# Every third half chunk's low part on GpSimd instead of VectorE, in a two-layer decoder trunk that streams all its weights

## The chip, the cores and the metric

One core of a Trainium2 chip. The metric is the device time of one execution in microseconds (us): the median of several runs, and beside it one profiled execution with its trace.

## The reference, cut to what matters

The program computes two layers on 256 tokens of width 1024, in float32. Layer 0 mixes with an RG-LRU group and an HGRN2 group, layer 1 with a Mamba-2 scan; each layer then has cross-attention into 256 memory tokens and a squared-ReLU MLP. Nearly all of the arithmetic is products with weights:

```
h = rmsnorm(x, norm_mix_g[l])
proj = h @ e_w_in[e]            (layer 0, 1024 x 6144; layer 1: o_w_in, 1024 x 6176)
x = x + mix                     (mix = ... @ e_w_out[e], 2048 x 1024)
x = x + mem_cross_attn(...)     (four 1024 x 1024 weights)
hf = rmsnorm(x, norm_ffn_g[l])
x = x + jnp.square(jax.nn.relu(hf @ ffn_w1[l])) @ ffn_w2[l]
```

Each weight is used once, against all 256 tokens.

## The kernel before, in words

**Three products for one.** A float32 operand is split into two parts that TensorE takes in a shorter format: the high part is the operand rounded, the low part is what the rounding left. Activations have parts H and L, weights `wh` and `wl`. A product is three matmuls: `wh`x`H`, `wh`x`L`, `wl`x`H` (lines 465, 467, 468 where the weights are the stationary operand, 484 to 486 where the activations are; 1202 to 1204 for the last four halves).

**The weight stream.** The host lays all weights out as 161 chunks of 2048 columns by 128 partitions, in the order in which they are used. Each is loaded and split as two halves of 1024 columns, so there are 322 halves, numbered h = 0 to 321 (the two of chunk `dt` have 512 columns). Class `Stream` takes each half through three steps:

- `loading` (line 155): SyncE's queue issues the DMA of 512 KB into `raw`, of which there are 4 buffers.
- `splitting`, line 169: ScalarE copies `raw` with rounding into `wh`, of which there are 5 buffers.
- `splitting`, line 170: VectorE subtracts `wh` from `raw` into `wl`, of which there are 5 buffers. Both operands lie in SBUF. When this is done the `raw` buffer is free. Halves 0 to 2 are split in two pieces each, so line 170 issues 325 instructions.

When TensorE's products of half h have been written, `ahead` (lines 183 to 188) writes the splits up to half h + 3 and the loads up to h + 7; the buffers allow one more split, since a half can be copied as soon as the half five before it is used up.

**What else VectorE does.** Line 629 is a causal convolution (its input is in PSUM), 1057, 1090, 1088, 1093, 1111, 1112 and 1126 belong to the Mamba-2 scan of one of eight groups, 359 and 388 make low parts of activations, 730 and 731 belong to HGRN2. Lines 303 to 308 are a chain of small instructions for an inverse square root; 316 and 318 turn its result into two diagonal matrices `dgh` and `dgl`, which TensorE multiplies with ones (line 326) to spread the scale over the partitions. The chain of lines 1015 to 1024 (a softplus and a cumulative sum) makes `acT` for the scan, which TensorE transposes at line 1033.

**What sets the order.** The program text gives an order and priorities (the chains above run under `high_priority`); a scheduler writes one fixed list of instructions per engine from it. Each engine works through its own list in order and waits at semaphores. An instruction that stands early in TensorE's list and whose operand is late stops everything behind it.

GpSimd does little: four constants and two memsets (line 673) at the start.

Of the kernel before, what the change touches and what calls it, by code (L numbers as in the profile page):

```python
# [7 lines left out]
F32 = mybir.dt.float32  # L8
# [4 lines left out]
ALU = mybir.AluOpType  # L13
# [117 lines left out]
class Stream:  # L131
# [26 lines left out]
    def splitting(self):  # L158
        h = self.cut
        self.cut += 1  # L160
        nc = self.nc
        hk, n = self._shape(h)
        w = hk * n
        raw = self.raw.pop(h)
        hi = self.pool.tile([P, 1024], F32R, tag="wh", bufs=PART_BUFS, name=f"wh{h // 2}_{h % 2}")
        lo = self.pool.tile([P, 1024], F32R, tag="wl", bufs=PART_BUFS, name=f"wl{h // 2}_{h % 2}")
        self.parts[h] = tuple(t[:, :w].rearrange("p (k c) -> p k c", k=hk) for t in (hi, lo))
        for a, b in self._pieces(h, w):
            self.last = nc.scalar.copy(hi[:, a:b], raw[:, a:b])  # L169
            nc.vector.tensor_tensor(lo[:, a:b], raw[:, a:b], hi[:, a:b].bitcast(F32), ALU.subtract)  # L170
            yield

    def load(self, upto):
# [1128 lines left out]
```

## Time and profile before

| | us |
|---|---|
| median of 3 runs (lowest, highest) | 1012.09 (1011.84, 1013.56) |
| the profiled execution's own time | 1005.65 |
| its span, first to last instruction | 1003.8 |
| TensorE busy | 990.7 |
| VectorE busy | 773.6 |
| ScalarE busy | 615.0 |
| GpSimd busy | 1.2 |

The profiled execution lies 6.4 us under the median; 1.85 us of it lie outside its span. TensorE's busy time is a union of overlapping matmuls, so what it lost inside small waits does not all show as idle. Its granted clock is 0.996 over the span.

### The profile page before, as it was taken

The page shows a single profiled execution, that of the slowest core. Times are in us where ns is not written, and L with a number is a line of the kernel's source. Part 1 is how long each engine was busy: PE and PEld are TensorE (multiplying, and loading weights), DVE is VectorE, ACT ScalarE, POOL GpSimd, SP SyncE. Part 2 cuts the span into 40 slices and gives each one's busy share as a digit, 9 for nine tenths or more (in the row PEclk, how much of TensorE's full clock was granted, in tenths as well). Part 3 has the DMA queues.
Part 4 walks back from the last instruction along what each step waited for, and adds up shares of the span by engine and source line. Part 5 has one row for each costly group of instructions (what it writes and reads, how often), then busy time and mean ns, then how long its engine had stood idle before and what let it go on. Part 6 is the DMA issues. An engine that isn't in the chain of part 4 may idle for free.

```text
span 1003.8 us, 20814 instructions
## 1 busy us (share of the span) xinstructions
PE 990.7 (99%) x8453; PEld 942.1 (94%) x8453; DVE 773.6 (77%) x1459; ACT 615.0 (61%) x907; POOL 1.2 (0%) x6
## 2 busy tenths in 40 slices
PE   9999999999999999999999999999999999999997
PEld 8898998989999999999998999999999999989985
DVE  7968888796887864675798888999989777656653
ACT  6667868775566554455445867778456657535542
POOL 0000000000000000000000000000000000000000
PEclk9999999999999999999999999999999999999999
DMA  8765453545544655555555655554646345666551
GB/s 294 274 218 164 127 188 123 176 148 183 187 147 159 197 190 191 196 198 194 168 172 194 217 196 189 188 156 141 211 137 200 127 159 184 198 192 191 192 188 42
DMA packets 52703, 180.54 MB, mean 180 GB/s; under 512 B 5984, under 2 KB 6144, under 8 KB 52480
## 3 DMA queue, kind: packets, MB, share of 16 engines
q1 hardware_dynamic: 52176, 178.41, 53.9%
q8 instruction: 66, 1.08, 0.4%
q10 hardware_dynamic: 432, 0.80, 0.2%
q14 instruction: 29, 0.24, 0.1%
HBM read 178.11 MB, written 1.08 MB: 179 GB/s over the span
## 4 chain that ended last, share of the span: by engine, by line
PE 84%; DVE 10%; ACT 3%; DMA 2%; issue 1%; SPq 0%; ACTq 0%; DVEq 0%
PE pg L465 20%; PE pg L467 19%; PE pg L468 19%; PE pg L484 6%; PE pg L486 6%; PE pg L485 5%; DVE wl L170 3%; DMA raw<-in_wst_dram 1%; ACT wh L169 1%; DVE cv L629 1%; PE pm L689 1%; PE pm L851 1%; PE pm L852 1%; PE pm L853 1%; DMA mem<-in_memT_dram 1%
## 5 line engine op out<-in xcount | busy, mean ns | idle before, releaser
L169 ACT CAST wh<-raw 128x1024 fp32r<-128x1024 f32 (+1 forms) x325 | 337.0, 1041 | 301.3 <-PE pg L467 205.3
L170 DVE TENSOR_TENSOR wl<-raw,wh 128x1024 fp32r<-128x1024 f32 (+1 forms) x325 | 391.5, 1211 | 164.1 <-ACT wh L169 163.3
L465 PE MATMUL pg<-nh,wh 128*128 128x256 f32 x1280 | 359.6, 281 | 0.0
L467 PE MATMUL pg<-nl,wh 128*128 128x256 f32 x1280 | 355.9, 278 | 0.0
L468 PE MATMUL pg<-nh,wl 128*128 128x256 f32 x1280 | 355.8, 278 | 0.0
L465 PEld LDWEIGHTS pg<-nh,wh 128*128 128x128 f32 x1280 | 241.1, 188 | 1.5 <-issue 0.7
L468 PEld LDWEIGHTS pg<-nh,wl 128*128 128x128 f32 x1280 | 241.3, 189 | 0.0
L467 PEld LDWEIGHTS pg<-nl,wh 128*128 128x128 f32 x1280 | 240.9, 188 | 0.4
L465 PE MATMUL pg<-yh,wh 128*128 128x256 f32 x768 | 215.6, 281 | 0.6 <-ACT wh L169 0.6
L467 PE MATMUL pg<-yl,wh 128*128 128x256 f32 x768 | 214.7, 280 | 0.1
L468 PE MATMUL pg<-yh,wl 128*128 128x256 f32 x768 | 214.3, 280 | 0.0
L465 PEld LDWEIGHTS pg<-yh,wh 128*128 128x128 f32 x768 | 146.1, 190 | 1.8 <-ACT wh L169 1.5
L467 PEld LDWEIGHTS pg<-yl,wh 128*128 128x128 f32 x768 | 145.7, 190 | 0.4 <-DVE yl L388 0.3
L468 PEld LDWEIGHTS pg<-yh,wl 128*128 128x128 f32 x768 | 145.4, 189 | 0.6 <-DVE wl L170 0.5
L486 PE MATMUL pg<-wl,yh 128*128 128x512 f32 x176 | 69.3, 394 | 0.0
L485 PE MATMUL pg<-wh,yl 128*128 128x512 f32 x176 | 69.0, 392 | 0.0
L484 PE MATMUL pg<-wh,yh 128*128 128x512 f32 x176 | 68.7, 391 | 0.0
L629 DVE SCALAR_TENSOR_TENSOR cv<-pg,smC,cv 128x255 f32<-128x255 f32 (+2 forms) x96 | 39.9, 478 | 0.7 <-ACT cv L626 0.7
L484 PEld LDWEIGHTS pg<-wh,yh 128*128 128x128 f32 x176 | 33.0, 188 | 7.4 <-issue 0.3
L485 PEld LDWEIGHTS pg<-wh,yl 128*128 128x128 f32 x176 | 33.1, 188 | 7.2
L486 PEld LDWEIGHTS pg<-wl,yh 128*128 128x128 f32 x176 | 33.1, 188 | 6.7
L943 DVE SCALAR_TENSOR_TENSOR t<-pg,rb 128x512 f32<-128x512 f32 x32 | 21.9, 690 | 13.2 <-PE pg L468 13.0
(266 smaller groups left out, 1105.7 us busy)
## 6 DMA issues: line engine op xcount, KB each, us to landing
raw<-in_wst_dram SPq DMA_DIRECT2D x317, 512.0 KB, 3.7
ac<-acd SPq DMA_DIRECT2D x16, 256.0 KB, 4.5
mem<-in_memT_dram SPq DMA_DIRECT2D x8, 256.0 KB, 4.2
raw<-in_wst_dram SPq DMA_DIRECT2D x8, 256.0 KB, 4.9
xres<-in_xT_dram SPq DMA_DIRECT2D x4, 256.0 KB, 5.8
gw<-in_gatew_dram SPq DMA_DIRECT2D x1, 1024.0 KB, 5.5
gn<-in_fing_dram SPq DMA_DIRECT2D x2, 256.0 KB, 3.7
out_dram<-o SPq DMA_DIRECT2D x2, 256.0 KB, 2.1
```

What stands on the lines that cost most here:

```text
L169: self.last = nc.scalar.copy(hi[:, a:b], raw[:, a:b])
L170: nc.vector.tensor_tensor(lo[:, a:b], raw[:, a:b], hi[:, a:b].bitcast(F32), ALU.subtract)
L465: PE.matmul(o[:, j, :], wh[:, cs], xh, start=(first and k == 0 and j == 0), stop=False, skip_group_check=True)
L467: PE.matmul(o[:, j, :], wh[:, cs], xl, start=False, stop=False, skip_group_check=True)
L468: PE.matmul(o[:, j, :], wl[:, cs], xh, start=False, stop=(last and k == kt - 1), skip_group_check=True)
L484: PE.matmul(os[j], h, wh, start=(first and k == 0), stop=False)
L485: PE.matmul(os[j], lo, wh, start=False, stop=False)
L486: PE.matmul(os[j], h, wl, start=False, stop=(last and k == kt - 1))
L629: V.scalar_tensor_tensor(r[:, j, i:], o[:, j, :256 - i], col(wn, (3 - i) * stride + c), r[:, j, i:], ALU.mult, ALU.add)
L689: PE.matmul(tgt[32 * j:32 * j + 32, b // 4, :], Kf[:, 32 * b:32 * b + 32], qq[:, 32 * b:32 * b + 32], start=True, stop=True, tile_position ...
L851: PE.matmul(o, ah, bh, start=(i == 0), stop=False)
L943: V.scalar_tensor_tensor(t, o, 0.0, b2(n.rb), ALU.max, ALU.mult)
```

## The change

Of every half with h > 8 and h divisible by 3, the subtraction that makes the low part is issued on GpSimd instead of VectorE. These are h = 9, 12, ..., 321, that is 105 of the 322 halves, all of them 1024 columns wide. Nothing else is written differently; the scheduler makes new lists from it. One line is added, so all later lines have numbers one higher.

```diff
         for a, b in self._pieces(h, w):
             self.last = nc.scalar.copy(hi[:, a:b], raw[:, a:b])
-            nc.vector.tensor_tensor(lo[:, a:b], raw[:, a:b], hi[:, a:b].bitcast(F32), ALU.subtract)
+            e = nc.gpsimd if h > 8 and h % 3 == 0 else nc.vector
+            e.tensor_tensor(lo[:, a:b], raw[:, a:b], hi[:, a:b].bitcast(F32), ALU.subtract)
             yield
```

The lists move at other places too. Two of them follow, each for VectorE and TensorE. In the names, the number behind `wl_`, `wh_` or `pm_` is the buffer's number in the program and is the same before and after; `wl_0` and `wl_1` are the first and second half of a chunk.

**Place 1, the transposition of `acT` at the start of layer 1.** VectorE before, the end of the chain (lines 352 to 355) that leads to `acT`:

```order
L352 SCALAR_TENSOR_TENSOR sp_7671<-sp_7671,sp_7668 128x256 x2
L170 TENSOR_TENSOR wl_1_7853<-raw_1_7664,wh_1_7852 128x1024
L352 SCALAR_TENSOR_TENSOR sp_7671<-sp_7671,sp_7668 128x256 x4
L170 TENSOR_TENSOR wl_0_7886<-raw_0_7729,wh_0_7885 128x1024
L353 SCALAR_TENSOR_TENSOR sp_7671<-sp_7671,sp_7670 128x256
L629 SCALAR_TENSOR_TENSOR cv_7815<-pg_7740,smC,cv_7815 128x255
L355 SCALAR_TENSOR_TENSOR sp_7669<-sp_7671,sp_7669 128x256
```

VectorE now, the same chain (its lines are now 353 to 356, and `acT` is made at 1025):

```order
L351 TENSOR_SCALAR sp_7671<-sp_7668 128x256
L353 SCALAR_TENSOR_TENSOR sp_7671<-sp_7671,sp_7668 128x256 x6
L354 SCALAR_TENSOR_TENSOR sp_7671<-sp_7671,sp_7670 128x256
L356 SCALAR_TENSOR_TENSOR sp_7669<-sp_7671,sp_7669 128x256
L171 TENSOR_TENSOR wl_1_7853<-raw_1_7664,wh_1_7852 128x1024
L1022 TENSOR_SCALAR sp_7691<-sp_7669,na 128x256
L1025 SCALAR_TENSOR_TENSOR acT<-smB,sp_7691 128x128 x2
```

`wl_0_7886` and the convolution now stand behind the chain.

TensorE before, where the transposition (line 1033) stands in the products of chunk `z_0`, whose `wh_1_7768` is its second half:

```order
L468 MATMUL pg_7824<-nh_7461,wl_1_7769 128x256
L465 MATMUL pg_7824<-nh_7461,wh_1_7768 128x256
L467 MATMUL pg_7824<-nl_7462,wh_1_7768 128x256
L1033 MATMUL pm_7807<-smB,acT 128x32
L468 MATMUL pg_7824<-nh_7461,wl_1_7769 128x256
```

TensorE now, the same transposition (line 1034), with `wh_0_7725`, the first half of that chunk:

```order
L469 MATMUL pg_7740<-nh_7461,wl_1_7661 128x256
L466 MATMUL pg_7824<-nh_7359,wh_0_7725 128x256
L468 MATMUL pg_7824<-nl_7360,wh_0_7725 128x256
L1034 MATMUL pm_7807<-smB,acT 128x32
L469 MATMUL pg_7824<-nh_7359,wl_0_7726 128x256
```

It stands 40 rows earlier in TensorE's list (4012 instead of 4052).

**Place 2, the scale of group 5 of the scan (`dgh_10248`, `pm_10346`).** VectorE before, ahead of `dgh`:

```order
L170 TENSOR_TENSOR wl_1_10486<-raw_1_10225,wh_1_10485 128x1024
L306 SCALAR_TENSOR_TENSOR nt_10236<-nt_10235 128x2
L170 TENSOR_TENSOR wl_0_10524<-raw_0_10285,wh_0_10523 128x1024
L307 TENSOR_TENSOR nt_10236<-nt_10236,nt_10234 128x2
L170 TENSOR_TENSOR wl_1_10600<-raw_1_10344,wh_1_10599 128x1024
L308 SCALAR_TENSOR_TENSOR nt_10235<-nt_10236,nt_10235 128x2
L359 TENSOR_TENSOR kv_11139<-vN_8340,kv_11138 128x512
L316 TENSOR_SCALAR dgh_10248<-smB,nt_10235 128x128 x2
```

VectorE now (303 to 308 are 304 to 309, 316 is 317):

```order
L308 TENSOR_TENSOR nt_10236<-nt_10236,nt_10234 128x2
L1112 SCALAR_TENSOR_TENSOR y_10321<-cv_9773,smB,pm_10309 128x256
L309 SCALAR_TENSOR_TENSOR nt_10235<-nt_10236,nt_10235 128x2
L1113 TENSOR_TENSOR y_10321<-y_10321,z_9974 128x512
L317 TENSOR_SCALAR dgh_10248<-smB,nt_10235 128x128 x2
L319 SCALAR_TENSOR_TENSOR dgl_10249<-smB,nt_10235,dgh_10248 128x128 x2
L336 TENSOR_TENSOR ysq_10354<-ysq_10354 128x256
L360 TENSOR_TENSOR kv_11139<-vN_8340,kv_11138 128x512
```

`wl_1_10486` (h = 231) is on GpSimd now; `wl_0_10524`, `wl_1_10600`, `kv_11139` and one `ysq` stand behind `dgh`. TensorE before, where the products with ones (line 326) stand in chunk `oo_02`:

```order
L468 MATMUL pg_10292<-yh_9096,wl_0_10406 128x256
L465 MATMUL pg_10292<-yh_9096,wh_0_10405 128x256
L326 MATMUL pm_10346<-dgh_10248,onesr 128x256
L1081 MATMUL pm_10376<-cv_10184 128x256
L326 MATMUL pm_10346<-dgl_10249,onesr 128x256
```

TensorE now, in chunk `oo_00`:

```order
L468 MATMUL pg_10290<-yl_9819,wh_1_10221 128x256
L469 MATMUL pg_10290<-yh_9818,wl_1_10222 128x256
L327 MATMUL pm_10346<-dgh_10248,onesr 128x256
L1082 MATMUL pm_10376<-cv_10184 128x256
L327 MATMUL pm_10346<-dgl_10249,onesr 128x256
```

They stand 77 rows earlier (5318 instead of 5395). The same products of groups 6 and 7 stand 71 and 86 rows earlier.

## Rows read from the trace of the kernel before

**Rows 1.** The page's head and its busy times of the engines.

```profile
span 1003.8 us, 20814 instructions
...
PE 990.7 (99%) x8453; PEld 942.1 (94%) x8453; DVE 773.6 (77%) x1459; ACT 615.0 (61%) x907; POOL 1.2 (0%) x6
```

**Rows 2.** Busy time by stretch; columns are named in the first row.

```profile
core 0: us, PE busy (x) PEld busy (x) DVE busy (x) ACT busy (x) POOL busy (x), PEclk, DMA share, GB/s
300.00:500.00 200.00, 200.00 (x1756) 200.00 (x1755) 133.99 (x167) 107.91 (x139) 0.00 (x0) 1.00 0.57 189
500.00:525.00 25.00, 24.61 (x212) 24.21 (x212) 23.70 (x59) 12.12 (x17) 0.00 (x0) 1.00 0.46 151
525.00:550.00 25.00, 23.68 (x173) 22.44 (x172) 22.61 (x51) 13.51 (x19) 0.00 (x0) 0.93 0.60 199
625.00:775.00 150.00, 148.50 (x1277) 143.53 (x1276) 142.03 (x327) 98.78 (x143) 0.00 (x0) 1.00 0.53 169
```

**Rows 3.** Waits of the whole span: total us, times, longest us.

```profile
ACT wh L169 <- PE pg L467: 205.3, 157, 3.4
DVE wl L170 <- ACT wh L169: 163.3, 175, 3.3
...
PE pm L326 <- DVE dgh L316: 1.6, 6, 0.4
PE pm L1033 <- DVE acT L1024: 1.3, 1, 1.3
```

**Rows 4.** Timeline 400 to 412: start us, duration us, instruction, [idle before, releaser].

```profile
400.74 1.05 ACT L169 CAST wh<-raw 128x1024 fp32r<-128x1024 f32 x1 [1.67 <-PE pg L467]
...
401.83 1.23 DVE L170 TENSOR_TENSOR wl<-raw,wh 128x1024 fp32r<-128x1024 f32 x1 [0.29 <-ACT wh L169]
...
403.46 1.05 ACT L169 CAST wh<-raw 128x1024 fp32r<-128x1024 f32 x1 [1.67 <-PE pg L467]
```

**Rows 5.** Timeline 694 to 704, half 225: its copy, its low part, its first use.

```profile
694.20 1.05 ACT L169 CAST wh<-raw 128x1024 fp32r<-128x1024 f32 x1 [0.20 <-DMA raw<-in_wst_dram]
...
698.29 2.43 DVE L629 SCALAR_TENSOR_TENSOR cv<-pg,smC,cv 128x255 f32<-128x255 f32 x6 [0.68 <-ACT cv L626]
...
701.03 1.22 DVE L170 TENSOR_TENSOR wl<-raw,wh 128x1024 fp32r<-128x1024 f32 x1
...
703.35 0.28 PE L468 MATMUL pg<-nh,wl 128*128 128x256 f32 x1
```

**Rows 6.** Timeline, TensorE at the two places of the section on the change.

```profile
537.14 0.24 PE L1033 MATMUL pm<-smB,acT 32*128 32x32 f32 x1 [1.32 <-DVE acT L1024]
...
722.22 0.39 PE L326 MATMUL pm<-dgh,onesr 128*128 128x256 f32 x1 [0.40 <-DVE dgh L316]
```

**Rows 7.** Groups by form over the span: count, then busy us, mean ns of one.

```profile
L170 DVE TENSOR_TENSOR wl<-raw,wh 128x1024 fp32r<-128x1024 f32 x317 | 386.1, 1224 | 162.7 <-ACT wh L169 162.0
...
L673 POOL MEMSET st<- 128x512 f32 x2 | 1.0, 524 | 0.3 <-POOLq L1292 0.3
```

**Rows 8.** VectorE's groups by form from 625 to 775 us, same columns.

```profile
L170 DVE TENSOR_TENSOR wl<-raw,wh 128x1024 fp32r<-128x1024 f32 x47 | 57.4, 1225 | 2.0 <-ACT wh L169 1.9
L1090 DVE TENSOR_TENSOR E<-E,cbm 128x1536 f32<-128x1536 f32 x5 | 8.8, 1757 | 0.0
L629 DVE SCALAR_TENSOR_TENSOR cv<-pg,smC,cv 128x254 f32<-128x254 f32 x18 | 7.9, 479 | 0.0
...
L1126 DVE SCALAR_TENSOR_TENSOR y<-y,smB,rb 128x256 f32<-128x256 f32 x14 | 6.5, 481 | 0.0
...
L359 DVE TENSOR_TENSOR yl<-y,yh 128x512 fp32r<-128x512 f32 x7 | 4.8, 691 | 0.7 <-ACT yh L1129 0.7
L318 DVE SCALAR_TENSOR_TENSOR dgl<-smB,nt,dgh 128x128 fp32r<-128x128 f32 x15 | 4.6, 350 | 0.0
...
L1112 DVE TENSOR_TENSOR y<-y,z 128x512 f32<-128x512 f32 x6 | 4.2, 694 | 0.0
```

## The prediction

> **What bounds the kernel now.** I read the page's busy times first. TensorE is busy 990.7 of 1003.8 us, VectorE 773.6, GpSimd 1.2 [rows 1]. So the sum over the span says that TensorE sets the time and that work taken from VectorE was mostly hidden. What is left to win or to lose lies where TensorE waits for VectorE, and for that the stretches have to be told apart.
>
> The view of busy time by stretch [rows 2] shows two kinds. From 300 to 500 us TensorE is busy for all of 200 us and VectorE for 134; there the time of a low part matters to nobody. From 500 to 550 and from 625 to 775 us VectorE is busy for 23.7 and 22.6 of 25 and for 142.0 of 150 us, and TensorE for a little less than the stretch. These two are where a term can lie.
>
> The view of waits [rows 3] says the same from the other side. VectorE waited 163.3 us for the copies of line 169, and the copies waited 205.3 us for TensorE to give a weight buffer back: the splitting runs ahead and is held up by the buffers, not by its speed. TensorE's own waits for VectorE are small: 1.6 us in six places for `dgh`, 1.3 us in one for `acT`.
>
> How far ahead, the timeline shows [rows 4]. Copies stand 2.72 us apart, which is TensorE's time for one half (24 matmuls of 256 columns, so 0.113 us each). A copy starts when the half five before has been used up, so its half is needed 4 x 2.72 = 10.9 us later. The copy takes 1.05 and the low part 1.23 us, which leaves 8.6 us. At 694 us it looks otherwise [rows 5]: the copy of half 225 ends at 695.25, its low part stands in VectorE's list behind other work until 701.03, ends at 702.25, and TensorE takes it at 703.35, with 1.1 us to spare.
>
> **The change, part by part.** Removed from VectorE: 105 subtractions of 1.224 us [rows 7], 128.5 us in all. Between 300 and 500 us that is worth nothing, since TensorE never waited there. Added on GpSimd: 105 such subtractions, and each copy now has to signal another engine; on ScalarE and in the DMA queue nothing is added, and some loads of `ac` change places with a weight load in SyncE's list, at a DMA share of 0.46 to 0.60 [rows 2], which I cost at nothing. GpSimd's list holds nothing else, so a subtraction that waits there for its copy holds up no one but the matmuls that need it. A `raw` buffer of a moved half comes free later by what GpSimd takes longer; 8.6 us of cover hide that in the quiet stretches, and in the tight ones it is freed earlier than now, because half 225 waited 5.8 us for VectorE.
>
> *What GpSimd takes for one.* The trace has no operation with two operands on GpSimd. The lower bound is VectorE's own 1.22 us. For the upper one I take GpSimd's memset, 524 ns for 512 columns written [rows 7]: 1.05 us for 1024 columns of one stream, 3.1 us for three streams (two read, one written) one after another. I take two streams' worth, 2.1 us, in the middle. The Trainium skill (GPSIMD Engine Reference, Performance versus the Vector engine) gives 4497 ns for 2048 columns, from which 2.25 us would be an estimate; no row shows it yet.
>
> *What VectorE loses while GpSimd works.* Nothing in the trace shows it, as the two engines never work side by side on SBUF operands. The bounds are nothing, and the whole 2.1 us in which VectorE might stand still. Between them I choose by the mix of VectorE's instructions in the tight stretch [rows 8]: lines 170, 1090, 1126, 359, 318 and 1112 read two tensors from SBUF and sum to 86.3 of the 142.0 us, 61%; others, such as line 629, read one from PSUM. If two reads at once are what GpSimd leaves no room for, VectorE loses 0.61 x 2.1 = 1.3 us for each moved subtraction, a little more than the 1.22 it gains.
>
> That choice can be weighed against a rule. The Trainium skill (SBUF — State Buffer, Who interferes with whom) states that a VectorE instruction with two SBUF inputs and a GpSimd instruction that reads SBUF shut each other out for the whole of the one that came first. It speaks against this change; with 2.1 us lost instead of 1.3 my sum below would be +16.7 us instead of +9.6.
>
> *Place 1, `acT`.* Before, TensorE waited 1.3 us there [rows 6]. Its transposition now stands 40 rows earlier, 40 x 0.113 = 4.5 us. VectorE's list ahead of `acT` is shorter by three moved subtractions (h = 168, 171, 174), one that now stands behind it, and three convolutions of 0.44 us (7.9 us for 18 [rows 8]): 4 x 1.22 + 1.3 = 6.2 us. So without any loss to GpSimd the wait is 1.3 + 4.5 - 6.2, about nothing (-0.4). With 3 x 1.3 = 3.9 us lost it is 3.5 us, which is +2.2 us on what it was.
>
> *Place 2, the scale of group 5.* Before, TensorE waited 0.4 us [rows 6]. Its products now stand 77 rows earlier, 8.7 us. The last time that VectorE waited for another engine's result of any weight before `dgh` is at 698.29 [rows 5], so I count from there: three moved subtractions (h = 225, 228, 231), 3.7 us; two subtractions, one `kv` and one `ysq` that now stand behind, 2 x 1.22 + 1.1 = 3.5 us. Without loss the wait is 0.4 + 8.7 - 7.2 = 1.9 us; with 3 x 1.3 us lost it is 5.8, +5.4 on before. Groups 6 and 7 stand earlier by as much, but TensorE is then already late by this, so they add nothing.
>
> *The other chains.* Of the six places where TensorE waited for `dgh` [rows 3] four are left. A moved subtraction is there every 3 x 2.72 = 8.2 us; a chain of some 4 us meets one of 2.1 us in about 0.7 of cases and loses 1.3 us, against 0.4 us won by a third of a subtraction less: 4 x 0.5 = +2 us, from nothing to 7.
>
> Sum: 2.2 + 5.4 + 2.0 = +9.6 us. The profiled execution of 1005.65 would become 1015.3; the same added to the median of 1012.09, which is 6.4 us higher, is **1021.7 us**. At the upper bounds (3.1 us, all of it lost) the three terms are 3 x 3.1 - 1.7 = 7.6, 1.5 + 9.3 = 10.8 and 7, +25.4 us or 1037.5.
>
> **The rivals.** *Both engines read side by side.* Then VectorE loses nothing, and only its gain is left. TensorE's wait at place 1 goes (1.3 us) and with it the piece at half clock that follows: the granted clock is 0.93 from 525 to 550 us [rows 2], worth 0.07 x 25 = 1.7 us. Place 2 gives 1.5 us back, the other chains win 4 x 0.4 = 1.6. That is -3.1 us, 1009.0. For it: copies of ScalarE run beside VectorE's subtractions all the time, and those keep 1.22 us. Against it: that tells of ScalarE alone, and an operation with two operands on GpSimd has no row. With a loss of x us for each moved subtraction the three terms sum to 8.8 x - 1.8, and 1.7 less where the clock stays up; the sum is below -2 us where x is under 0.17, and there this rival decides. Chance 0.18.
>
> *The cover takes it.* By the same sum the change is within 2 us where x lies between about 0.2 and 0.4: place 1 then waits 0.8 us instead of 1.3 and keeps its clock, place 2 waits 3.1 instead of 0.4, the chains win half a microsecond, and the time is 1012 to 1013. For it speaks that GpSimd's subtractions may often fall where VectorE has no work or reads from PSUM, of which half the list around 698 us consists [rows 5]. Chance 0.14.
>
> *GpSimd is as dear as its upper bound.* With 3.1 us and 61% of it lost, 1.9 us for each, place 1 is 3.6, place 2 7.2 and the chains 4: +15 us, 1027. The moved low parts themselves would still be in time: half 225 would end at 695.25 + 3.1, before the 703.35 at which it is used [rows 5]. Chance 0.16. That the change does not do what it says is no case, as GpSimd's list holds the 105 subtractions.
>
> **How the numbers follow.** The forecast has 0.52: it needs a loss near the middle of the bounds and an order that is too early for it. The range goes from the first rival to most of the way to the upper bounds, 1008.5 to 1034.0; below it lie a few cases in which VectorE also sheds its half-empty waits, above it those where all bounds are high together, 15 in 100 in sum. Faster by over 0.2% (2 us, about what a measurement of this kernel can tell from no change) is the first rival, 0.18. The second rival is within it, 0.14. The forecast and the third rival are slower, 0.68.
>
> **What would show it.** GpSimd: 105 subtractions in the trace of after, 2 to 3 us each. VectorE: its instructions with two SBUF tensors, line 171 above all, should have a longer mean than 1.22 us or idle time in front of them that ends with GpSimd, while line 630 keeps its 0.48; VectorE's busy time falls by less than 128 us. TensorE: waits of some us at line 1034 and at line 327 near 715 us, and a granted clock below 1.0 behind each. From 300 to 500 us nothing should change. The prediction is wrong if line 171 keeps 1.22 us on VectorE beside a working GpSimd, or if TensorE's waits do not grow although it does not.

## The result and the profile after

The changed kernel takes 1042.24 us (median of 4 executions, 1041.54 to 1043.75) against 1011.97 before (1007.18 to 1013.56): **ratio 1.0344, 95% interval 1.0309 to 1.0379**. The forecast was 1021.7 us with a range of 1008.5 to 1034.0. The side was right, the size not, and the result lies above the range. The profiled execution took 1041.54 us; its span grew by 36.0 us. Executions of the kernel before lie up to 11.4 us apart, and two traces with the same list on TensorE (the change: 1734 matmuls in 198.0 us; run 2 below: 1699 in 199.9) differ by 3% in pace from 300 to 500 us at a granted clock of 1.00, so costs below are read from ratios with their intervals, or from waits at named places.

The page's head and busy times of after, against [rows 1]:

```profile
span 1039.8 us, 20923 instructions
...
PE 999.6 (96%) x8453; PEld 947.3 (91%) x8453; DVE 754.1 (73%) x1354; ACT 614.8 (59%) x907; POOL 265.1 (25%) x111
```

VectorE gave up 128.5 us of subtractions, but its busy time fell by only 19.5 (773.6 to 754.1). So 109 us came back as longer instructions: 1.04 us for each of the 105 moved ones. And yet VectorE does less than before while the kernel is slower, so it is not its throughput that sets the time.

Busy time by stretch, columns as in [rows 2] (the granted clock is the third number from the end; 1.00 is 2.4 GHz, and the other level is half of it):

```profile
500.00:525.00 25.00, 22.86 (x187) 22.67 (x186) 20.08 (x48) 9.39 (x14) 4.78 (x2) 0.93 0.48 153
525.00:550.00 25.00, 18.98 (x165) 18.58 (x164) 24.34 (x33) 12.30 (x16) 9.25 (x3) 1.00 0.48 154
550.00:575.00 25.00, 25.00 (x166) 23.38 (x167) 16.79 (x37) 18.10 (x24) 5.16 (x3) 0.87 0.65 209
...
725.00:750.00 25.00, 20.23 (x152) 19.20 (x150) 22.69 (x45) 12.08 (x17) 6.62 (x3) 0.86 0.45 148
```

TensorE stands for 6 us of 25 where `acT` is made (525 to 550) and for 5 where group 5's scale is made (725 to 750). Its granted clock is below 1.0 in or behind each (0.86 in the second stretch itself, 0.87 from 550 to 575). It is 0.93 from 500 to 525 too, where TensorE stands for 2 us.

Waits of TensorE over the span (total us, times, longest), against [rows 3]; a row for which [rows 3] has no counterpart, `nsq`, follows from before:

```profile
PE pm L327 <- DVE dgh L317: 13.7, 7, 4.8
PE pm L340 <- DVE nsq L336: 5.6, 5, 1.9
PE pm L1034 <- DVE acT L1025: 5.5, 1, 5.5
PE pg L468 <- DVE nl L389: 1.6, 2, 1.0
PE pm L690 <- DVE K L732: 1.5, 2, 0.8
```

```profile
PE pm L339 <- DVE nsq L335: 0.7, 1, 0.7
```

No row for a low part on GpSimd stands among them: the moved subtractions are in time. What is late are VectorE's chains, `dgh` at seven places and the sums of squares `nsq` at five.

The moved line on both engines (durations in ns: min/median/max):

```profile
L171 DVE TENSOR_TENSOR wl<-raw,wh x220: 684/1224/3108, 5.9 to 1017.3; 128x1024 fp32r<-128x1024 f32 x106, 128x512 fp32r<-128x512 f32 x4
...
L171 POOL TENSOR_TENSOR wl<-raw,wh x105: 2357/2404/3693, 29.0 to 1020.2; 128x1024 fp32r<-128x1024 f32 x105
```

On VectorE the same subtraction keeps its 1224 ns at the median and takes up to 3108. Three other groups by form, after and then before (for the convolution, line 630 now, see line 629 in [rows 8]):

```profile
L360 DVE TENSOR_TENSOR yl<-t,yh 128x512 fp32r<-128x512 f32 x32 | 33.0, 1031 | 14.8 <-ACT yh L949 14.8
...
L630 DVE SCALAR_TENSOR_TENSOR cv<-pg,smC,cv 128x255 f32<-128x255 f32 x32 | 14.2, 474 | 1.0 <-ACT cv L627 1.0
...
L305 DVE TENSOR_SCALAR nt<-nt 128x2 int32<-128x2 int32 x16 | 10.5, 656 | 0.3
```

```profile
L359 DVE TENSOR_TENSOR yl<-t,yh 128x512 fp32r<-128x512 f32 x32 | 22.1, 692 | 2.0 <-ACT yh L948 2.0
...
L304 DVE TENSOR_SCALAR nt<-nt 128x2 int32<-128x2 int32 x16 | 2.7, 167 | 0.2
```

The low part of an activation went from 692 to 1031 ns and the 128x2 instruction from 167 to 656. The convolution, whose input lies in PSUM, has not changed. So the others wait inside themselves.

How that makes TensorE late can be followed at group 5 (timeline, rows of one stretch):

```profile
729.88 2.62 POOL L171 TENSOR_TENSOR wl<-raw,wh 128x1024 fp32r<-128x1024 f32 x1 [3.80 <-ACT wh L169]
...
731.34 1.20 DVE L305 TENSOR_SCALAR nt<-nt 128x2 int32<-128x2 int32 x1
...
737.19 2.92 POOL L171 TENSOR_TENSOR wl<-raw,wh 128x1024 fp32r<-128x1024 f32 x1 [4.69 <-ACT wh L169]
...
737.83 2.30 DVE L307 SCALAR_TENSOR_TENSOR nt<-nt 128x2 f32<-128x2 f32 x1
...
742.25 0.55 PE L327 MATMUL pm<-dgh,onesr 128*128 128x256 f32 x1 [4.77 <-DVE dgh L317]
```

Two instructions on two columns take 1.20 and 2.30 us and end where GpSimd's subtraction ends (732.5 and 740.1). Both belong to the chain to `dgh`, for which TensorE has then been waiting 4.77 us. Alone, such an instruction took 0.16 to 0.17 us before, so these two account for 3.2 us of the delay.

### The profile page after: what moved, and what is told of

Its sections match the earlier page's. It is cut to its first block, busy times and chain, and to the rows that moved or that the text cites. A ratio compares the mean times of both kernels' runs of the same rounds, so it can differ in the third digit from the quotient of the medians.

```text
span 1039.8 us, 20923 instructions
## 1 busy us (share of the span) xinstructions
PE 999.6 (96%) x8453; PEld 947.3 (91%) x8453; DVE 754.1 (73%) x1354; ACT 614.8 (59%) x907; POOL 265.1 (25%) x111
## 4 chain that ended last, share of the span: by engine, by line
PE 73%; DVE 18%; issue 3%; ACT 3%; DMA 1%; SPq 0%; ACTq 0%; DVEq 0%
PE pg L466 17%; PE pg L468 17%; PE pg L469 17%; PE pg L485 5%; PE pg L487 5%; PE pg L486 5%; DVE wl L171 4%; DVE cv L630 2%; DMA raw<-in_wst_dram 1%; ACT wh L169 1%; DVE nl L389 1%; DVE nsq L405 1%; DVE E L1058 1%; DVE E L1091 1%; PE pm L853 1%
## 5 line engine op out<-in xcount | busy, mean ns | idle before, releaser
L171 POOL TENSOR_TENSOR wl<-raw,wh 128x1024 fp32r<-128x1024 f32 x105 | 263.9, 2514 | 756.9 <-ACT wh L169 685.9
L171 DVE TENSOR_TENSOR wl<-raw,wh 128x1024 fp32r<-128x1024 f32 (+1 forms) x220 | 272.2, 1240 | 148.5 <-ACT wh L169 147.8
L360 DVE TENSOR_TENSOR yl<-t,yh 128x512 fp32r<-128x512 f32 x32 | 33.0, 1031 | 14.8 <-ACT yh L949 14.8
```

Source lines behind the costliest of these rows:

```text
L171: e.tensor_tensor(lo[:, a:b], raw[:, a:b], hi[:, a:b].bitcast(F32), ALU.subtract)
L360: V.tensor_tensor(lo, src, h.bitcast(F32), ALU.subtract)
```

## The experiments

In the expectations "lists" are the engines' instruction lists. Ratios are to the kernel before on the same chip (median 1006.1 to 1009.1 us).

**1. Everything stays on VectorE, and GpSimd works beside it.** The lists of before (on VectorE two subtractions change places):

```diff
+            nc.vector.tensor_tensor(lo[:, a:b], raw[:, a:b], hi[:, a:b].bitcast(F32), ALU.subtract)
             if h > 8 and h % 3 == 0:
+                nc.gpsimd.tensor_tensor(raw[:, a:b], raw[:, a:b], hi[:, a:b].bitcast(F32), ALU.subtract)
```

> VectorE makes every low part as before, and GpSimd makes the same subtraction once more for the 105 halves, into the raw buffer, where nobody reads it; TensorE's and VectorE's lists are those of before. Theory 'blocking' (VectorE stands still while GpSimd reads SBUF): VectorE loses about 1 us for each of the 105 as it did with the change, and is relieved of nothing, so TensorE waits at the same chains and more: 1045 to 1070 us. Theory 'lists' (the loss comes from the transposition and the scale products standing 40 and 77 rows earlier in TensorE's list): the lists are the old ones, 1012 to 1016 us. Theory 'late parts' (TensorE waits for low parts that GpSimd delivers late): nobody waits for GpSimd's results here, 1012 to 1016 us.

Measured: 1083.76 us, ratio 1.0733 (1.0678 to 1.0789). Waits of TensorE:

```profile
PE pm L328 <- DVE dgh L318: 14.6, 8, 3.5
PE pm L1035 <- DVE acT L1026: 6.4, 1, 6.4
```

With nothing moved, the old order and no low part made by GpSimd, the same chains are late, `dgh` at eight places and not seven, though not all of them the same. So GpSimd's work beside VectorE is enough to make such waits. The time came out above what I had set. Why is not shown; the mean granted clock was 0.981, against 0.991 with the change.

**2. GpSimd writes without reading.** The order of the change on TensorE and VectorE:

```diff
             if h > 8 and h % 3 == 0:
+                nc.gpsimd.memset(lo[:, a:b].bitcast(F32), 0.0)
```

> The lists of the change, but for the 105 halves GpSimd writes zeros instead of subtracting, so it reads nothing (the low parts of these halves are left out of the result). 'Blocking' by reads: VectorE's instructions keep their durations of before, the relief is left, 1004 to 1012 us. 'Lists': the early slots wait as with the change, 1030 to 1042 us. 'Late parts': the memset is shorter than the subtraction and the parts come earlier, about 1012 us.

Measured: 1013.29 us, ratio 1.0063 (1.0034 to 1.0091), and two of the waits:

```profile
PE pm L329 <- DVE dgh L319: 1.5, 3, 0.9
...
PE pm L1036 <- DVE acT L1027: 1.1, 1, 1.1
```

The lists are those of the change, so the order alone does not make the waits.

**3 and 4. The change in the quiet and in the tight stretches alone.** Of the changed line its condition only:

```diff
-h > 8 and h % 3 == 0
+h % 3 == 0 and (104 <= h < 160 or 268 <= h)                      # run 3: 37 halves
+h > 8 and h % 3 == 0 and not (104 <= h < 160 or 268 <= h)        # run 4: the other 68
```

> Only the 37 moved halves that lie in the stretches of the MLPs where TensorE waits for nothing (h from 104 to 159 and from 268 on). 'Blocking': VectorE is stopped there too, but no chain that TensorE waits for runs there and a low part has 8 us of cover: 1010 to 1014 us. 'Late parts': with 8 us of cover also 1010 to 1014. A cost for each moved half, wherever it stands, would show 37/105 of the loss, 1022 us.

> The other 68 moved halves, the quiet ones stay on VectorE. 'Blocking' and 'lists': the whole loss, 1039 to 1043 us. A cost for each moved half: 68/105 of it, 1032 us.

Measured: 1004.62 us, ratio 0.9977 (0.9939 to 1.0015), for the 37; 1049.26 us, ratio 1.0394 (1.0326 to 1.0461), for the 68. In run 3 VectorE's busy time is 743.0 us, where 37 subtractions less would leave 728.3: it lost 0.40 us for each there too, and that cost nothing that can be measured. The whole loss is in the stretches with chains. Run 4 came out above the 1039 to 1043 us that I had set; its waits are those of the change (`dgh` 12.8 us, `acT` 5.5, `nsq` 5.4), its mean granted clock is lower (0.983), and its interval contains the change's 1.0344.

**5. GpSimd's subtraction in four pieces.**

```diff
+                for c in range(a, b, 256):
+                    nc.gpsimd.tensor_tensor(lo[:, c:c + 256], raw[:, c:c + 256], hi[:, c:c + 256].bitcast(F32), ALU.subtract)
```

> The lists of TensorE and VectorE are those of the change; only GpSimd's subtraction of a moved half is cut into four of 256 columns. If the two engines shut each other out one instruction at a time, VectorE gets in after a quarter of a subtraction (some 0.6 to 0.8 us in place of 2.4): the longest of its instructions fall from 3.1 us to under 2, TensorE's waits at the chains to about half, and the ratio to before from 1.034 to between 1.005 and 1.02. If GpSimd keeps VectorE out for as long as it has work in its list, nothing is gained, and the fixed cost of four instructions for one makes it worse: 1.034 to 1.05.

Measured: 1031.37 us, ratio 1.0246 (1.02 to 1.0292).

```profile
L174 DVE TENSOR_TENSOR wl<-raw,wh x220: 684/1225/1778, 5.8 to 1007.0; 128x1024 fp32r<-128x1024 f32 x106, 128x512 fp32r<-128x512 f32 x4
```

```profile
PE pm L330 <- DVE dgh L320: 8.5, 6, 3.0
PE pm L1037 <- DVE acT L1028: 5.2, 1, 5.2
```

GpSimd now works for 345.6 us and not 265.1, and still the loss is smaller. VectorE's longest subtraction takes 1.78 us and not 3.11: it gets in between the pieces, so it is kept out by one instruction at a time. The gain is less than I had set, and the wait for `acT` has hardly fallen, which is not explained.

**6. Kinds of VectorE instructions beside kinds of GpSimd instructions.** A kernel of its own; in each row VectorE runs 6 to 40 instructions of one kind on its own operands, and GpSimd none or three of another:

```diff
+            V.tensor_tensor(vo[:, :2], gt, vb[:, :2], ALU.mult)
+            G.tensor_tensor(go[:, :2], vo[:, :2], gb[:, :2], ALU.mult)
+            for _ in range(3):
+                g(go)      # g: tensor_tensor of two, tensor_copy of one, or memset, 128x1024
+            for _ in range(n):
+                v(vo)      # v: tensor_tensor of two, with one in PSUM, tensor_scalar; 1024, 512 or 2 columns
```

> A kernel of its own, which computes none of the reference: rows of one kind of VectorE instruction, alone and beside three 128x1024 instructions of GpSimd that read two tensors, one, or none (a memset). If any read of SBUF by GpSimd shuts out any instruction of VectorE whose inputs all lie in SBUF, then the longest 128x1024 subtraction, the longest TENSOR_SCALAR and the longest 128x2 instruction beside GpSimd's subtraction all take about 2.4 us more than alone, those with one operand in PSUM take what they take alone, and beside the memset all do. If only instructions with two SBUF tensors are stopped, TENSOR_SCALAR and the 128x2 TENSOR_SCALAR keep their times. If the two only share a rate, no instruction has 2.4 us more, but all of a row are longer by a like share.

Groups by form, with busy us and mean ns; the names give VectorE's kind, then GpSimd's (`two`, `one` or `set` for what it does, `none` for nothing; `vts` is TENSOR_SCALAR, `vpsum` has one operand in PSUM, `vtiny` works on two columns). One execution:

```profile
L241 DVE TENSOR_SCALAR vts_gtwo<-va 128x1024 f32<-128x1024 f32 x12 | 14.4, 1198 | 0.7 <-POOL gtwo_vts L265 0.3
...
L235 DVE TENSOR_TENSOR vtwo_gtwo<-va,vb 128x1024 f32<-128x1024 f32 x6 | 13.4, 2235 | 0.5 <-POOL gtwo_vtwo L265 0.3
L247 DVE TENSOR_SCALAR vtiny_gtwo<-va 128x2 f32<-128x2 f32 x40 | 12.9, 322 | 1.6 <-POOL gtwo_vtiny L265 0.3
...
L241 DVE TENSOR_SCALAR vts_gset<-va 128x1024 f32<-128x1024 f32 x12 | 10.6, 880 | 0.7 <-POOL gset_vts L265 0.3
...
L250 POOL TENSOR_TENSOR gtwo_vtwo<-ga,gb 128x1024 f32<-128x1024 f32 x3 | 9.8, 3260 | 0.2
L235 DVE TENSOR_TENSOR vtwo_gone<-va,vb 128x1024 f32<-128x1024 f32 x6 | 9.5, 1584 | 0.5 <-POOL gone_vtwo L265 0.3
...
L241 DVE TENSOR_SCALAR vts_gnone<-va 128x1024 f32<-128x1024 f32 x12 | 8.3, 694 | 0.4
...
L238 DVE TENSOR_TENSOR vpsum_gnone<-pp,vb 128x512 f32<-128x512 f32 x12 | 8.3, 691 | 0.4
L238 DVE TENSOR_TENSOR vpsum_gtwo<-pp,vb 128x512 f32<-128x512 f32 x12 | 8.3, 691 | 0.7 <-POOL gtwo_vpsum L265 0.3
...
L235 DVE TENSOR_TENSOR vtwo_gset<-va,vb 128x1024 f32<-128x1024 f32 x6 | 7.3, 1225 | 0.5 <-POOL gset_vtwo L265 0.3
L235 DVE TENSOR_TENSOR vtwo_gnone<-va,vb 128x1024 f32<-128x1024 f32 x6 | 7.3, 1225 | 0.2
L250 POOL TENSOR_TENSOR gtwo_vpsum<-ga,gb 128x1024 f32<-128x1024 f32 x3 | 7.0, 2349 | 0.2
...
L247 DVE TENSOR_SCALAR vtiny_gnone<-va 128x2 f32<-128x2 f32 x40 | 6.8, 170 | 1.4
```

Beside three subtractions of GpSimd a row of VectorE is longer by 13.4 - 7.3 = 6.1 us for the subtraction, 14.4 - 8.3 = 6.1 for TENSOR_SCALAR and 12.9 - 6.8 = 6.1 for the 128x2 one: **2.0 us for each GpSimd subtraction, whichever of these three stands beside it**, paid by one instruction of VectorE: in each row the trace has three longer ones, and the others keep their time. GpSimd is held too: its subtraction takes 3.26 us on average beside VectorE's, and 2.35 beside the instructions with an operand in PSUM. Those lose nothing (691 and 691 ns). One read on GpSimd (a copy) costs VectorE 0.7 us, and a memset nothing beside a subtraction, but 0.8 us beside TENSOR_SCALAR. That last one I had not expected.

The Trainium skill (SBUF — State Buffer, Who interferes with whom) tells these cases apart in the same way: two SBUF inputs conflict with GpSimd's reads only, a fast two-port mode such as TENSOR_SCALAR's with any use, and other instructions with one SBUF input not at all. This run agrees with it in each kind tried (2.0 us beside a subtraction, 0.8 for TENSOR_SCALAR beside a memset, nothing with an operand in PSUM).

**7. One read on GpSimd, in the kernel.**

```diff
+                nc.gpsimd.tensor_copy(lo[:, a:b], raw[:, a:b])
```

> The lists of the change, but GpSimd copies raw into wl (one tensor read) and does not subtract the high part, so the low parts of 105 halves are wrong by that part. If every read of SBUF by GpSimd stops VectorE, the loss goes with the time that GpSimd is busy: with copies of 1.2 to 2 us the ratio is 1.012 to 1.03 and the lines 359, 388 and 730 stay well over their times of before. If only two reads at once do it, the ratio is that of the memset, 1.00 to 1.008.

Measured: 1018.02 us, ratio 1.0087 (1.0052 to 1.0122). It lies between what the two theories set. An instruction of half the length (1.17 us on average) brings a quarter of the loss. That it costs VectorE a third as much (0.7 against 2.0 us in run 6) and more often ends before TensorE needs the chain's result would explain this; it is not shown by itself.

**8 and 9. The two places of the prediction, left out, and alone.** Again the condition only:

```diff
-h > 8 and h % 3 == 0
+h > 8 and h % 3 == 0 and not (160 <= h < 178 or 216 <= h < 234)  # run 8: 93 halves
+h % 3 == 0 and (160 <= h < 178 or 216 <= h < 234)                # run 9: 12 halves
```

> As the change, but the 12 halves around the two places of the prediction (162 to 177 and 216 to 231) stay on VectorE; 93 are moved. If the loss is at the many other chains, as the delays by place of the change suggest (+36 us in all, of them some 6 at acT and 10 at group 5), about 20 us are left: ratio 1.016 to 1.024, with waits under 2 us at the two places. If the two places and what follows from them carry it, as the prediction had it (7.6 of 9.6 us), the ratio is 1.000 to 1.008.

> Only the 12 halves at the two places of the prediction (162 to 177 and 216 to 231) go to GpSimd, the other 93 moved halves stay on VectorE: the counterpart of the run that left these 12 out and was 1.0239. If losses at places add up, this one is the rest of the 1.0344: 1.008 to 1.016, with a wait of about 5 us for acT and one of about 5 for dgh. If the two places cost what the prediction's terms for them said (2.2 + 5.4 us), it is 1.006 to 1.009. If the waits there need halves moved elsewhere as well, it is within 1.000 to 1.004.

Run 8: 1030.67 us, ratio 1.0239 (1.0198 to 1.028). Run 9: 1024.38 us, ratio 1.0167 (1.0126 to 1.0207). Waits of run 8 (from its shortest execution, 1024.2 us), then of run 9:

```profile
PE pm L340 <- DVE nsq L336: 6.0, 5, 2.5
PE pm L327 <- DVE dgh L317: 5.7, 7, 1.8
...
PE pm L1034 <- DVE acT L1025: 0.4, 1, 0.4
```

```profile
PE pm L1034 <- DVE acT L1025: 5.0, 1, 5.0
PE pm L327 <- DVE dgh L317: 4.0, 8, 2.3
...
PE pm L327 <- DVE dgl L319: 2.2, 1, 2.2
```

Both are well above zero. The twelve subtractions around the two places cost some 17 us, and the 93 others 24. The sum, 4.1%, is a little over the change's 3.4%; the scheduler makes other lists in both, so they need not add up. By run 8 "the two places carry it" falls. Run 9 lies a little above the 1.016 that I had set for losses that add up, and it is half a miss in its waits: I had expected a wait of about 5 us for a `dgh` as well as for `acT`, but group 5 waits only 0.19 us there (at 727.8), and the longest waits for `dgh` and `dgl` are at 506 and 708 us. So the 4.8 us at group 5 are not owed to these twelve alone; whether other moved halves or the change's lists make the rest is open.

**10. The change's order and VectorE's relief, with GpSimd idle.** For the 105 halves TensorE multiplies by `self.zero`, a tile of zeros:

```diff
+        low = h <= 8 or h % 3
+        lo = self.pool.tile([P, 1024], F32R, tag="wl", bufs=4, name=f"wl{h // 2}_{h % 2}") if low else self.zero
...
+            if low:
+                nc.vector.tensor_tensor(lo[:, a:b], raw[:, a:b], hi[:, a:b].bitcast(F32), ALU.subtract)
```

> The low part of the 105 halves is left out altogether: TensorE multiplies by a tile of zeros instead, GpSimd does nothing, and the lists of TensorE and VectorE are those of the change. So it has the change's order and VectorE's relief without anything on GpSimd. If the earlier places in TensorE's list cost by themselves, waits of 1 us and more remain at acT and dgh and the ratio is 1.003 to 1.008. If they do not, it is 0.994 to 1.001, since VectorE has 128 us less to do; by the prediction's own terms without any loss it would be 3 us under before, 0.997. Then all of the loss of the change, and what the memset had more than before, comes from GpSimd.

```profile
PE pm L1037 <- DVE acT L1028: 1.0, 1, 1.0
...
PE pm L330 <- DVE dgh L320: 0.6, 3, 0.2
```

Measured: 1009.30 us, ratio 1.0005 (0.9977 to 1.0033). Order and relief together change nothing that can be measured: the interval allows a gain of 0.2% and a loss of 0.3%. What the change loses comes from GpSimd's subtractions, and there was next to nothing to win. Run 3 is equal to the kernel before, and run 10 bounds what a better place for the low parts could give.

## Why the prediction was right in its side and wrong in its size

- **What bounds the kernel:** right. TensorE sets the time, VectorE's throughput does not matter, and the loss lies in the stretches with chains (runs 3, 4 and 10). The sign that nothing would change from 300 to 500 us did not hold quite: TensorE stands there for 2.0 us, in three waits before 340 us.
- **GpSimd's time for one:** taken as 2.1 us, measured 2.40 at the median, and 2.35 beside instructions that it does not meet (run 6, `gtwo_vpsum`). The estimate of 2.25 us that the prediction drew from the Trainium skill (GPSIMD Engine Reference, Performance versus the Vector engine) was nearer.
- **What VectorE loses:** taken as 1.3 us for each, measured 1.04 on average. The choice by the mix of operands was a fair mean, but a mean was the wrong quantity. Run 6 shows that one instruction stands still for 2.0 us, or none does; where that one belongs to a late chain, up to the whole of it is on the path. The mix also counted only instructions with two tensors in SBUF, and run 6 holds TENSOR_SCALAR as much.
- **Place 1:** predicted +2.2 us, the wait grew from 1.3 [rows 3] to 5.5, +4.2. **Place 2:** predicted +5.4, it grew from 0.40 [rows 6] to 4.8, +4.4. Together 8.6 against 7.6. The sum of the two held, but partly by luck: place 1 came out at nearly twice its term and place 2 below it, and the working is off in both. Without any loss the prediction left nothing at place 1 and 1.9 us at place 2; run 10 has 1.0 and at most 0.2.
- **The other chains: this is the step that failed.** It read "+2 us, from nothing to 7". In after the first three rows of waits sum to 24.8 us, with `nl` and `K` to 27.9. Before, `dgh`, `acT` and `nsq` waited 1.6 + 1.3 [rows 3] + 0.7 us = 3.6. Of the 24.3 us between, 8.6 belong to the two places, so the other chains cost **15.7 us** in waits. Run 8 puts all that the 93 other halves bring at 20 to 28 us, the clock and smaller waits with it. The prediction counted only four places, out of those where TensorE already waited. Of the five that [rows 3] has outside place 2, just one grew by over 0.1 us, from 0.22 to 2.14 (at 515 us). The others are new: groups 1, 2 and 6 of the scan wait 1.73, 1.97 and 2.38 us for `dgh`, though the prediction had groups 6 and 7 add nothing, and four norms wait for `nsq` where before there was no wait. A place where TensorE does not wait yet has a **lead**, the time from the end of the chain to the matmul that takes its result, and that may be less than one GpSimd instruction. The first norm is such a place. Before (timeline):

```profile
35.07 0.43 DVE L335 TENSOR_TENSOR nsq<-nsq 128x256 f32<-128x256 f32 x1
...
36.32 0.50 PE L339 MATMUL pm<-smB,nsq 128*128 128x1 f32 x4
```

After:

```profile
34.66 2.39 POOL L171 TENSOR_TENSOR wl<-raw,wh 128x1024 fp32r<-128x1024 f32 x1 [3.23 <-ACT wh L169]
...
35.03 3.11 DVE L171 TENSOR_TENSOR wl<-raw,wh 128x1024 fp32r<-128x1024 f32 x1
...
38.06 0.41 DVE L336 TENSOR_TENSOR nsq<-nsq 128x256 f32<-128x256 f32 x1
...
38.53 0.61 PE L340 MATMUL pm<-smB,nsq 128*128 128x1 f32 x4 [1.94 <-DVE nsq L336]
```

  The lead was 36.32 - 35.50 = 0.8 us, and no view of waits shows it. VectorE's own subtraction, which stands ahead of `nsq`, took 3.11 us beside GpSimd's, and TensorE waited 1.94. Of the 16 places where products need a `dgh`, 13 had a lead under 2 us before, from the end of the second `dgh` instruction to the first matmul on it. A short lead is not enough by itself: with the change 6 of the 13 waited over 0.2 us, and one more whose lead had been 2.05. The trace of before had the leads; the prediction went by the waits.
- **The clock:** in no term of the sum; only the first rival priced it, as a gain of 1.7 us. By the stretches shown above, TensorE loses (0.07 + 0.13 + 0.14) x 25 = 8.5 us to it after, and 0.07 x 25 = 1.8 before [rows 2], which is **+6.7 us** as an upper estimate, since part of the piece at half clock around group 5 falls into the wait itself. That it would fall behind the long waits the prediction's last part had said, without a price. With the waits' 24.3 us that makes 31.0 of the 36.0; the rest lies in shorter gaps and has not been assigned.
- **The rivals:** *Both engines read side by side* falls (run 6), and *the cover takes it* holds in the quiet stretches alone (run 3). *GpSimd is as dear as its upper bound* falls by its duration (2.40 us at the median, not 3.1), though the 1027 us that it gave were nearer to the result; its place 1 should read 3 x 1.9 - 1.7 = 4.0 us by its own terms and not 3.6, which leaves its sum at +15. Had VectorE lost nothing, the first rival set -3.1 us; run 10, which comes nearest to that case, gives between -2 and +3.
- **The rule weighed against the row:** what the Trainium skill (SBUF — State Buffer, Who interferes with whom) states of an exclusive lock was right in kind, as run 6 shows; the sum that the prediction made with it, +16.7 us, stays too small for the same missing places.

## What to carry to other kernels

Before work goes to GpSimd, list the **leads** of every chain on VectorE that TensorE depends on, not only the waits: each lead shorter than one GpSimd instruction is a place that can pay, for every such instruction that meets the chain, up to the time that it holds VectorE (2.0 us in run 6), less the lead. A mean loss for each instruction says nothing of this, and the sum of busy times even points the wrong way (VectorE's fell by 19.5 us here). If GpSimd must do such work, put it where there is no chain (run 3: no loss that can be measured), or cut it into pieces (run 5: 2.5% lost and not 3.4).

## What the runs showed of the hardware that was not expected

An instruction on 128x2 elements can take 2.2 us beside a GpSimd subtraction where alone it takes 0.17 (run 6; 2.30 us at group 5): it is held for 2.0 us, as long as one on 128x1024. TENSOR_SCALAR with one SBUF input is held as much as a subtraction with two, and by a memset as well (0.8 us), while a multiplication with one operand in PSUM is not held at all. That the memset run was slower than run 10 (1.0063 against 1.0005) fits this, but the two ran on different chips, and it is not shown.
